# Explicit places for recurrence steps, evacuations and side work, and the x sums of the first half on GpSimd, in a retention and HGRN2 inference step

## The chip, the cores and the metric

The kernel runs on one core of a Trainium2 chip. The metric is the device time of one execution in microseconds (us), median over several; the profile comes from one execution. TensorE (PE; PEld is its weight load) multiplies matrices, VectorE (DVE), ScalarE (ACT) and GpSimd (POOL) work element by element, SyncE (SP) only issues DMAs. Each engine runs its own instructions in one fixed order and waits on semaphores for the others.

## The reference

One layer on 2048 prompt tokens (and 8 single-token samples with stored states): normalise, project to eight groups of 512 columns, run four retention heads and four HGRN2 heads of 128 x 128 state, gate, project back, add the input, normalise.

```python
h = rmsnorm(x, norm_g)
p = (h @ w_in).astype(jnp.float32)
rq, rk, rv, rg, hq, hf, hi, hgate = jnp.split(p, 8, axis=-1)
rq, rk = rotary(rq, pos), rotary(rk, pos) * RET_DK ** -0.5
o_ret, s_ret_new = chunked_decay_recurrence(rq, rk, rv, log_gamma, s_ret)    # S = g S + k v, o = S q
o_ret = head_rmsnorm(o_ret, ret_g) * silu(rg)
logf = logaddexp(log(lb), log1p(-lb) + log_sigmoid(hf));  kin = (1 - lb) * sigmoid(-hf)
o_hg, s_hg_new = chunked_decay_recurrence(silu(hq), kin, hi, logf, s_hg)     # one decay per key row
o_hg = head_rmsnorm(o_hg, hg_g) * silu(hgate)
y = rmsnorm(x + concatenate([o_ret, o_hg], -1) @ w_out, final_norm_g)
```

All matrix products with weights are in float32 by two parts each: a high part that TensorE takes exactly and the low rest; high x high, high x low and low x high are added.

## The kernel before, in words

**Products.** Big matrix products are done in 2 x 2 blocks by a scheme of Strassen's kind with seven products per unit (`SLOTS`: A11, S1, S2, S4, A12, S3, A22 against B11, T1, T2, B22, B21, T3, T4). One product is 4 x 3 = 12 matmuls of 128x128 by 512 columns. S are sums of blocks of the one operand, T sums of blocks of the other.

**Units and positions.** Time is counted in positions; unit `u` begins at position 7u, and each whole position holds one product in two halves (the last product of a unit stands at 9, in the next unit). After a start in plain form, units -6 to -1 make V (values, stored to `v_dram`). Units 0 to 23 are the scan: H, G, R in turn (HGRN forget gate and query; both gates; retention key and query) for heads 0 to 3, first for tokens 0 to 1023 (units 0 to 11), then for 1024 to 2047. Units 24 to 31 are the output projection O, 256 tokens each. So three scan units, 21 positions, belong to one head of each kind. Units 0 to 11 write their split weights for H and R to `w_dram`; units 12 to 23 read them back (`w_reload`).

**x.** In V the normalised tokens are one operand in blocks (`tok_ops`: normalise, split in high and low, sums S1 to S4). For the scan they are the other operand: 1024 tokens as B11, B21, B12, B22 and T1 to T4. B11 and B21 stay from the last V units; `x12_load`, `x_norm`, `x_t1` to `x_t4` load and normalise the other 512 tokens once more and make T1 to T4 and B22 on VectorE with ScalarE's high parts. For the second half (`x1_*`) this is done in small steps during the first half and kept in `x_dram`, from which `swap_load` and `x_split` fetch it; the output weights' sums (`wo_*`, `t_dram`) likewise.

**Recurrences.** An H or R unit is followed by its recurrence over 8 chunks of 128 tokens. HGRN (`hgrn_rec`): `scores0`, `scores(1)`, `scores(3)`, `scores3` build the score matrix A level by level (TensorE's small matmuls, then `update` on VectorE, `keep`'s copies on ScalarE, the next `update`). Both kinds then share `tail_steps`, with g = 0, 1 for four chunks each: `kt` transposes keys, `uu` makes the state updates, `oo` the outputs (then four squares on ScalarE with accumulated sums, `rsqrt_mean` on GpSimd, four scalings on ScalarE into `ob`), `tr` transposes `ob`, multiplies by the gate on VectorE and stores to `o_dram`. Tiles `A`, `st`, `ks` and `ob` have one buffer each, `ps_lv` and `ps_o` two banks.

**Order.** `at(pos, f)` collects all steps, which are sorted by position and emitted. This order is binding for TensorE alone (`manual_schedule` with TensorE); for the other engines and the DMA queues a planner chooses at build time, by its own estimates, which instruction goes next. Recurrence steps are spread over a stretch by weights:

```python
for n, w in enumerate(ws):
    s += w
    at(7 * u + lo + (hi - lo) * s / total + 0.25, lambda n=n: get(n))
```

with 11.5 to 20.0 for HGRN (weights total 13.9) and 11.3 to 17.8 for retention (5.6). Work tiles of 128x512 come from a list of 12 (`t_get`, `t_done`), split weights from a ring of 6 (`r_get`, `r_done`); both lists hand out what was freed longest ago.

Of the kernel before, what the change touches and what calls it, by code (L numbers as in the profile page):

```python
# [18 lines left out]
P = 128  # L19
# [20 lines left out]
N_OB = 1  # L40
# [6 lines left out]
def step_kernel(ctx, tc, a, out):  # L47
# [27 lines left out]

    ident = const.tile([P, P], F32, name="ident")
# [4 lines left out]
    pool.memset(mhalf, -0.5)  # L81

# [6 lines left out]
    warm = const.tile([P, 1], F32, name="warm")  # L89
    act.activation(warm, zero[:, 0:1], AF.Sigmoid)  # L90
# [13 lines left out]
    lbd = const.tile([P, NH], F32, name="lbd")  # L104
    lb = const.tile([P, NH], F32, name="lb")
    lb1 = const.tile([P, NH], F32, name="lb1")
    lmask = const.tile([P, len(SMALL) * 16], U8, name="lmask")
    rs_all = const.tile([P, T // P], F32, name="rs_all")
    rsd = const.tile([NB, 2], F32, name="rsd")
# [26 lines left out]
    t_tag = {}  # L136

    def t_get(shape, name, dtype=F32):
        if not t_free:
            raise RuntimeError(f"{name}: " + " ".join(str(t[1].tensor.name) for t in t_tag.values()))  # L140
        tag = t_free.pop(0)
        t = tp.tile(shape, dtype, tag=tag, name=name)
        t_tag[id(t)] = (tag, t)
        return t
# [14 lines left out]
    V_ORDER = [4, 5, 6, 7, 2, 3, 0, 1]  # L159
# [36 lines left out]
    def stats(i):  # L196
        p = V_ORDER[i]
        ms = sm.tile([P, 4], F32, tag="ms", name=f"ms{p}")
        for j in range(2):
            c = 2 * p + j  # L200
            for h in range(2):
                r = t_get([P, GW], f"xn{c}{h}")
                sp.dma_start(r, a["x_prompt"][0, c * P : (c + 1) * P, h * GW : (h + 1) * GW])
                act.activation(r, r, AF.Square, accum_out=ms[:, 2 * h + j : 2 * h + j + 1])  # L204
                t_done(r)
        pool.tensor_tensor(ms[:, 0:2], ms[:, 0:2], ms[:, 2:4], op=ALU.add)  # L206
        rsqrt_mean(rs_all[:, 2 * p : 2 * p + 2], ms[:, 0:2], D, EPS)
# [20 lines left out]

    def tok_ops(i):
        r0, r1 = xr[i]  # L230
        rb = spread_to[i]
        for j, r in enumerate((r0, r1)):
            for k in range(4):
                kk = 4 * j + k
                dve.scalar_tensor_tensor(  # L235
                    r[:, k], r[:, k], g_in[:, kk : kk + 1], rb, op0=ALU.mult, op1=ALU.mult
                )
            n = P if i < 6 and j == 0 else 2 * P
            at = slice((i % 2) * 256, (i % 2) * 256 + n)
            hi_lo(x0[j][0][:, :, at], x0[j][1][:, :, at], r[:, :, :n])  # L240
        a11, a21, a12, a22 = r0[:, :, :P], r0[:, :, P:], r1[:, :, :P], r1[:, :, P:]
        s1, s2, s3, s4 = (t_get([P, 4, P], f"{n}_{i}") for n in ("S1", "S2", "S3", "S4"))
        dve.tensor_tensor(s1, a21, a22, op=ALU.add)
        dve.tensor_tensor(s2, s1, a11, op=ALU.subtract)
        dve.tensor_tensor(s3, a11, a21, op=ALU.subtract)
        dve.tensor_tensor(s4, a12, s2, op=ALU.subtract)
        sraw[i] = dict(S1=s1, S2=s2, S3=s3, S4=s4)

    sraw = {}

    def s_split(i, n):
        t, src = r_get(f"s{i}{n}"), sraw[i][n]
        split_raw(t, src.rearrange("p k t -> p (k t)"))
        t_done(src)
# [201 lines left out]
    r4 = {}  # L456

    def x12_load(kp):
        r4[kp] = rawp.tile([P, 2, 512], F32, tag="raw", name=f"xr1{kp}")
        for j in range(2):  # L460
            sp.dma_start(r4[kp][:, :, j * 256 : j * 256 + 256], a["x_t"][2 + j, :, 2 * kp : 2 * kp + 2])

    def blk_dg(blk, dg):
        dve.tensor_tensor(
            dg, ident.unsqueeze(1).to_broadcast([P, 4, P]),
            rs_all[:, 4 * blk : 4 * blk + 4].unsqueeze(2).to_broadcast([P, 4, P]), op=ALU.mult,
        )

# [5 lines left out]

    xs_box = {}

    def x_dg():
        xs_box["dg"] = t_get([P, 4, P], "dgb1")
        blk_dg(1, xs_box["dg"])

    def x_spread():
        xs_box["rb"] = t_get([P, GW], "rbb1")
        blk_spread(1, xs_box["dg"], xs_box["rb"])
        t_done(xs_box["dg"])

    def x_norm(kp):
        for j in range(2):
            k = 2 * kp + j
            dve.scalar_tensor_tensor(
                r4[kp][:, j], r4[kp][:, j], g_in[:, k : k + 1], xs_box["rb"], op0=ALU.mult, op1=ALU.mult  # L490
            )
# [21 lines left out]

    def x_block(b, src):
        h, l = x_tile(b, "x")
        halves(lambda kk, n: hi_lo(h[:, kk], l[:, kk], src[n]))

    def x_t1():
        b11 = [t.bitcast(F32) for t in X["B11"]]
        halves(lambda kk, n: sub(r4[n], r4[n], b11[1][:, kk]))  # L520
        halves(lambda kk, n: sub(r4[n], r4[n], b11[0][:, kk]))
        x_block("T1", r4)

    def x_t2():
        for n in range(2):
            sub(r4[2 + n], r4[2 + n], r4[n])
        x_block("T2", [r4[2], r4[3]])

    def x_t3():
        b11 = [t.bitcast(F32) for t in X["B11"]]  # L530
        halves(lambda kk, n: sub(r4[n], r4[2 + n], b11[0][:, kk]))
        halves(lambda kk, n: sub(r4[n], r4[n], b11[1][:, kk]))
        x_block("T3", r4)

    def x_t4():
        b21 = [t.bitcast(F32) for t in X["B21"]]
        halves(lambda kk, n: sub(r4[2 + n], b21[1][:, kk], r4[2 + n]))
# [1034 lines left out]
```

## Time and profile before

| what | value |
| --- | --- |
| median of 3 runs | 1182.38 us (1181.15 to 1185.52) |
| the profiled execution's own time | 1185.04 us |
| its span, first to last instruction | 1183.3 us |
| mean granted TensorE clock | 0.951 |
| DMA | 226.71 MB, mean 192 GB/s |

In the profile a group's line gives the source line, the engine, the operation, the tile written and the tiles read, shapes, count, then busy time and the mean duration, then the idle time of the engine just before these instructions and what ended it. "PE poth L884 <- ACT obh L876: 22.4, 8, 6.4" says that TensorE waited 22.4 us in 8 times, at most 6.4, before it wrote `poth` in line 884, until ScalarE's `obh` of line 876 was there. Names ending in h belong to HGRN, in r to retention.

### The profile page before, as it was taken

How to read it: one execution, taken by the hardware profiler on the slowest of the kernel's cores; microseconds unless marked ns; L12 is line 12 of the kernel's file. 1: busy time of each engine (PE TensorE's matmuls, PEld its weight loads, DVE VectorE, ACT ScalarE, POOL GpSimd, SP SyncE). 2: the span in 40 equal slices, each digit the busy share in tenths (PEclk: the TensorE clock that was granted, in tenths of full speed). 3: DMA queues.
4: the chain of work that ended last, by engine and by line, in shares of the span. 5: the costliest groups of instructions: out<-in, count | busy, mean ns of one | idle time of the engine just before them, and what ended most of it. 6: DMA issues, size and time to landing. Idle time of an engine off the chain costs nothing.

```text
span 1183.3 us, 22553 instructions
## 1 busy us (share of the span) xinstructions
PE 1070.9 (91%) x8696; PEld 867.4 (73%) x8696; DVE 786.1 (66%) x1366; ACT 579.8 (49%) x1316; POOL 233.6 (20%) x379
## 2 busy tenths in 40 slices
PE   9999996998898899889799979879998799999997
PEld 7777884777766777677677758657786677778886
DVE  7767598676666666677676446635655468977774
ACT  7745353555445455455574435425444448543342
POOL 2401000023122222312102112111211411031111
PEclk9999997998999999999989989979998899999999
DMA  8554445277456736755786654765564179544431
GB/s 308 198 170 146 140 160 186 105 263 266 153 198 237 255 140 236 254 184 179 284 277 193 209 195 154 221 200 191 170 225 146 30 233 322 193 131 166 152 125 71
DMA packets 126555, 226.71 MB, mean 192 GB/s; under 512 B 11200, under 2 KB 67648, under 8 KB 124656
## 3 DMA queue, kind: packets, MB, share of 16 engines
q1 hardware_dynamic: 104496, 150.52, 39.8%
q0 software_dynamic: 21808, 74.50, 16.5%
q8 instruction: 68, 1.11, 0.4%
q14 instruction: 39, 0.32, 0.1%
q10 hardware_dynamic: 144, 0.26, 0.1%
HBM read 141.81 MB, written 83.43 MB: 190 GB/s over the span
## 4 chain that ended last, share of the span: by engine, by line
PE 45%; DMA 16%; DVE 13%; issue 12%; POOL 6%; ACT 5%; SPq 1%; DVEq 0%; POOLq 0%; ACTq 0%
PE aO L689 6%; PE aH L689 5%; PE aV L689 4%; DMA g_dram<-g 3%; PE aG L689 3%; PE eO L689 3%; PE aR L689 3%; DMA dv<-vd_dram 2%; DMA wo<-in_w_out 2%; PE eG L689 2%; PE eH L689 2%; PE eV L689 2%; PE bO L689 2%; PE bR L689 1%; DMA xn<-in_x_prompt 1%
## 5 line engine op out<-in xcount | busy, mean ns | idle before, releaser
L973 ACT ACTIVATE qh<-kh 128x1024 f32<-128x1024 f32 x24 | 25.5, 1061 | 45.6 <-DVE kh L961 45.6
L961 DVE TENSOR_TENSOR kh<-kh,fph 128x512 f32<-128x512 f32 x48 | 33.0, 687 | 6.0 <-PE plh L1038 2.8
L868 PE MATMUL poh<-sth,qt 128*128 128x128 f32 x112 | 24.0, 297 | 14.1 <-DVE sth L859 14.0
L1226 DVE TENSOR_TENSOR dv<-dv,dk 128x512 f32<-128x512 f32 x16 | 11.0, 690 | 38.2 <-DMA dv<-vd_dram 38.1
L1342 DVE SCALAR_TENSOR_TENSOR xro<-xro,yms,fg 128x1024 f32<-128x1024 f32 (+1 forms) x17 | 20.7, 1222 | 22.9 <-POOL yms L117 21.5
L884 PE MATMUL poth<-ident,obh 128*128 128x128 f32 x64 | 15.4, 349 | 22.4 <-ACT obh L876 22.4
L876 ACT ACTIVATE obr<-por,orsr 128x128 f32<-128x128 f32 x64 | 18.2, 368 | 35.5 <-POOL orsr L117 35.5
L204 ACT ACTIVATE xn<-xn 128x512 f32<-128x512 f32 x32 | 20.0, 625 | 30.4 <-DMA xn<-in_x_prompt 27.4
L763 POOL DMA_DIRECT2D g_dram<-g x32 | 17.4, 542 | 86.5 <-DVE g L762 84.8
L1333 ACT ACTIVATE yj<-xro 128x512 f32<-128x512 f32 x32 | 20.3, 633 | 28.8 <-DVE xro L509 28.0
L872 ACT ACTIVATE obh<-poh 128x128 f32<-128x128 f32 x64 | 16.7, 275 | 34.9 <-PE poh L868 19.2
L964 DVE TENSOR_TENSOR qt<-qt,fph 128x512 f32<-128x512 f32 x48 | 33.1, 689 | 0.0
L235 DVE SCALAR_TENSOR_TENSOR xr<-xr,g_in,prs 128x256 f32<-128x256 f32 x48 | 19.8, 476 | 19.2 <-PE prs L224 19.2
L761 ACT ACTIVATE sg<-g 128x512 f32<-128x512 f32 x32 | 20.1, 628 | 25.2 <-DVE g L509 24.8
L884 PEld LDWEIGHTS poth<-ident,obh 128*128 128x128 f32 x64 | 9.9, 162 | 30.1 <-ACT obh L876 25.9
L206 POOL TENSOR_TENSOR ms<-ms 128x2 f32<-128x2 f32 x8 | 10.5, 1314 | 100.3 <-ACT xn L204 100.3
L868 PEld LDWEIGHTS poh<-sth,qt 128*128 128x128 f32 x112 | 18.0, 202 | 15.8 <-DVE sth L859 15.8
L762 DVE SCALAR_TENSOR_TENSOR g<-g,pk,sg 128x512 f32<-128x512 f32 x32 | 23.9, 748 | 6.3 <-ACT sg L761 5.8
L876 ACT ACTIVATE obh<-poh,orsh 128x128 f32<-128x128 f32 x64 | 18.2, 368 | 17.6 <-POOL orsh L117 17.6
L916 PE MATMUL par<-qr,kr 128*128 128x128 f32 x128 | 18.0, 285 | 9.6 <-DVE qr L509 9.6
L916 PEld LDWEIGHTS par<-qr,kr 128*128 128x128 f32 x128 | 17.1, 198 | 12.4 <-DVE qr L509 10.9
L866 PE MATMUL poh<-vh,A 128*128 128x128 f32 x128 | 25.5, 287 | 0.4
(1607 smaller groups left out, 3818.7 us busy)
## 6 DMA issues: line engine op xcount, KB each, us to landing
xn<-in_x_prompt SPq DMA_DIRECT2D x32, 256.0 KB, 4.0
v_dram<-vo SPq DMA_DIRECT2D x32, 256.0 KB, 4.1
g_dram<-g POOLq DMA_DIRECT2D x32, 256.0 KB, 4.5
xro<-in_x_prompt SPq DMA_DIRECT2D x16, 512.0 KB, 3.3
out_y_prompt<-xro POOLq DMA_DIRECT2D x15, 512.0 KB, 3.0
xr<-in_x_t SPq DMA_DIRECT2D x12, 512.0 KB, 4.7
t_dram<-wo POOLq DMA_DIRECT2D x20, 256.0 KB, 3.2
vh<-v_dram SPq DMA_DIRECT2D x16, 256.0 KB, 3.4
```

What stands on the lines that cost most here:

```text
L689: pe.matmul(ps, w[i], x[j], start=(first and k == 0 and m == 0), stop=(k == 3 and m == 2), skip_group_check=True,)
L762: dve.scalar_tensor_tensor(y, y, ng[:, hd : hd + 1], sg, op0=ALU.mult, op1=ALU.mult)
L866: pe.matmul(po[:, j], s_ctx["A"][:, c], box["v"][g][:, j], start=True, stop=src is None)
L868: pe.matmul(po[:, j], qcol(c), src, start=False, stop=True)
L876: act.activation(ob[:, j], po[:, j], AF.Copy, scale=rs[:, j : j + 1])
L884: pe.transpose(pt[:, j], box["ob", g][:, j], ident)
L916: pe.matmul(pa[:, j], k[:, cc], q[:, cc], start=True, stop=True)
L961: dve.tensor_tensor(kv[:, :, 0, :], kv[:, :, 0, :], two[:, :, 1:2].to_broadcast([P, nb, b]), op=ALU.mult)
L964: dve.tensor_tensor(qv[:, :, 1, :], qv[:, :, 1, :], two[:, :, 0:1].to_broadcast([P, nb, b]), op=ALU.mult)
L973: act.activation(kept_k, k, AF.Copy)
L1333: act.activation(jk, xro[c][:, (LO, HI)[n]], AF.Square, accum_out=yms[c][:, n : n + 1])
L1342: dve.scalar_tensor_tensor(xro[c][:, cc], xro[c][:, cc], ms[:, 0:1], fgb["t"][:, cc], op0=ALU.mult, op1=ALU.mult)
```

## The change

1. All events go to a heap, and `after(d, f)` puts a later part of a step `d` positions behind it. The whole loop is emitted under `manual_schedule` for VectorE, ScalarE, GpSimd and SyncE as well: their instructions and DMAs go in the order of the source, that is, of the positions. (What stands ahead of the loop stays with the planner, except on TensorE.)
2. Recurrence steps get positions of their own (`REC`), HGRN over 12.0 to 28.6 and retention over 11.9 to 20.1; retention's scores come ahead of its key transposes. `kt` takes its bank from `ps_lv`. Roots, scalings, stores, gates, rotations and copies follow by `after`. `ob` has two buffers.
3. The blocks B12 and B22 of the first half's x are stored while V normalises them (`tok_spool`); `V_ORDER` ends with 0, 1, 2, 3 where it ended with 2, 3, 0, 1, so the first half's kept blocks are tokens 512 to 1023, and `TB = (1, 0)` swaps the token halves everywhere in the scan. GpSimd makes T1 to T4 in pieces of 128x512 in the last two V units (`blocks_sums`) and stores them to `x_dram`; `swap_load` fetches them from position -6.4 on, with splits from -3.6 to 7.3. `x12_load`, `x_dg`, `x_spread`, `x_norm`, `x_block`, `x_t1` to `x_t4` go.
4. One of the ring's six buffers becomes two more work tiles when the scan opens; loads and side work (decode, x of the second half, output weights) get other positions; copies of unsummed output weights go from DRAM to DRAM (`wo_copy`, on SyncE's queue) and no longer from the work tile on GpSimd's queue.

```diff
-N_OB = 1
+N_OB = 2
+TB = (1, 0)
-    V_ORDER = [4, 5, 6, 7, 2, 3, 0, 1]
+    V_ORDER = [4, 5, 6, 7, 0, 1, 2, 3]
...
+    def at(pos, f):
+        count[0] += 1
+        heapq.heappush(ev, (pos, count[0], f))
+    def after(d, f):
+        at(now[0] + d, f)
...
+    def blocks_sums(i, n):
+        b11, b21 = (r[:, 2 * n : 2 * n + 2] for r in xr[i])
+        b12, b22 = (bs.pop((i, n, b)) for b in ("B12", "B22"))
+        t1, t2 = (t_get([P, 2, 256], f"b{t}{i}{n}") for t in ("T1", "T2"))
+        def put(b, t):
+            after(0.4, lambda: pool.dma_start(x_dram[X_NAMES.index(b), :, 2 * n : 2 * n + 2, slot(i)], t))
+            after(0.41, lambda: t_done(t))
+        def less(o, x, y):
+            pool.tensor_tensor(o, x, y, op=ALU.subtract)
+        less(t1, b12, b11)
+        put("T1", t1)
+        less(t2, b22, t1)
+        put("T2", t2)
+        less(b12, b22, b12)
+        put("T3", b12)
+        less(b22, b21, t2)
+        put("T4", b22)
...
     def scan_open():
+        big = wp.tile([P, 2, GW], F32, tag=free.pop(), name="big")
...
-            rsqrt_mean(rs, ms, P, eps)
-            for j in range(4):
-                act.activation(ob[:, j], po[:, j], AF.Copy, scale=rs[:, j : j + 1])
+            def root():
+                rsqrt_mean(rs, ms, P, eps)
+            def scale():
+                for j in range(4):
+                    act.activation(ob[:, j], po[:, j], AF.Copy, scale=rs[:, j : j + 1])
+            after(0.5, root)
+            after(1.0, scale)
...
-            update(li)
+            after(0.35, copies)
+            after(1.1, lambda: update(li))
...
-            for n, name in zip((-3.4, -2.4, -0.4, 0.6, 1.6, 2.6, 3.6), W_NAMES):
+            for n, name in zip((-3.4, -2.4, -1.4, -0.4, 0.6, 1.6, 2.6), W_NAMES):
                 at(U + n, lambda name=name: w_reload(u, name))
...
+    REC = {
+        0: (("s0", 12.0), ("s1", 14.8), ("s2", 17.6), ("load", 18.0), ("s3", 20.2), ("k0", 21.7), ("u0", 23.0),
+            ("k1", 23.2), ("o0", 23.9), ("u1", 24.3), ("o1", 25.1), ("last", 25.5), ("t0", 27.2), ("t1", 28.6)),
+        2: (("s0", 11.9), ("load", 12.0), ("s1", 12.7), ("k0", 13.3), ("u0", 14.3), ("k1", 14.5), ("o0", 15.5),
+            ("u1", 15.9), ("o1", 17.2), ("last", 17.6), ("t0", 18.8), ("t1", 20.1)),
+    }
-    REC_W = {
-        0: (0, 0.3, 2.3, 2.3, 2.3, 1.9, 0.9, 0.2, 0.5, 0.7, 0.9, 0.9, 0.7, 0),
-        2: (0, 0.3, 0.3, 0.6, 0.3, 0.3, 0.8, 0.6, 0.8, 0.8, 0.8, 0),
-    }
...
+    swap_events(0, "x0", dict(T1=-6.4, T2=-4.8, B22=-3.4, T3=-2.0, T4=-0.4),
+                dict(T1=-3.6, T2=-1.4, B22=0.8, T3=2.8, T4=6.8))
...
-        p0 = 84 + 7.2 + (0, 7.5, 14.2, 21.0, 28.5, 35.2, 42.0, 49.5)[hd]
-        at(p0, lambda hd=hd: d_load(hd))
+        p0 = 84 + 7.2 + (3.0, 10.2, 16.5, 21.9, 29.0, 35.5, 42.6, 49.5)[hd]
+        at(p0 - 2.5, lambda hd=hd: d_load(hd))
-    at(151.1, d_ms)
-    at(153.1, d_od)
+    at(158.0, d_ms)
+    at(163.1, d_od)
...
-    ev.sort(key=lambda e: e[:2])
-    for _, _, f in ev:
-        f()
+    with tc.manual_schedule(engines=ORDERED):
+        while ev:
+            now[0], _, f = heapq.heappop(ev)
+            f()
```

More of the change, by code (lines that the diff above doesn't have):

```diff
@@ L1 @@
+import heapq
 from contextlib import ExitStack
@@ L1142, in step_kernel, with wo_copy @@
     wd = {}
+    def wo_copy(k):
+        for b in ("B11", "B21", "B22"):
+            kh, n = int(b[1]) - 1, int(b[2]) - 1
+            sp.dma_start(
+                t_dram[X_NAMES.index(b), :, k], a["w_out"][(4 * kh + k) * P : (4 * kh + k + 1) * P, n * GW : (n + 1) * GW]
+            )
     def wo_load(k):
@@ L1150, in wo_sums, with put, store @@
     def wo_sums(k):
-        def put(b, t, keep=False):
-            pool.dma_start(t_dram[X_NAMES.index(b), :, k], t)
-            if not keep:
+        def put(b, t):
+            def store():
+                pool.dma_start(t_dram[X_NAMES.index(b), :, k], t)
                 t_done(t)
+            after(0.4, store)
         t1, t2 = t_get([P, GW], f"woT1{k}"), t_get([P, GW], f"woT2{k}")
-        put("B11", wd[0, 0], True)
-        put("B21", wd[1, 0], True)
-        put("B22", wd[1, 1], True)
         sub(t1, wd[0, 1], wd[0, 0])
         t_done(wd[0, 0])
-        put("T1", t1, True)
         sub(wd[0, 1], wd[1, 1], wd[0, 1])
@@ L1174, in swap_load @@
         x_tile(b, kind)
[L1175 removed]
+        sp.dma_start(raw(b), (t_dram if kind == "wo" else x_dram)[X_NAMES.index(b)])
     def flat(t):
```

452 lines of the change are left out of this document (236 added, 216 removed).

## The prediction

> **What bounds the kernel now.** I read the page first, then busy times by stage, then who waits for whom on TensorE, then the granted clock around one wait.
>
> ```profile
> span 1183.3 us, 22553 instructions
> PE 1070.9 (91%) x8696; PEld 867.4 (73%) x8696; DVE 786.1 (66%) x1366; ACT 579.8 (49%) x1316; POOL 233.6 (20%) x379
> PEclk9999997998999999999989989979998899999999
> ...
> ```
>
> TensorE is busy for 91% and no other engine for more than 66%: the time is TensorE's work, plus its idle time, plus whatever the low clock adds. By stage (V products and start; first and second half of the scan; output stage):
>
> ```profile
> 0.00:195.00 195.00, 181.69 (x826) 145.46 (x826) 148.13 (x252) 105.24 (x211) 27.93 (x38) 0.98 0.52 177
> 195.00:600.00 405.00, 359.12 (x3625) 289.63 (x3626) 272.75 (x493) 211.42 (x488) 96.91 (x163) 0.94 0.62 216
> 600.00:1030.00 430.00, 385.60 (x3590) 314.01 (x3589) 261.33 (x474) 207.34 (x486) 77.52 (x108) 0.94 0.61 196
> 1030.00:1184.00 154.00, 144.49 (x658) 118.36 (x656) 103.88 (x150) 55.81 (x132) 31.20 (x70) 0.98 0.39 131
> ...
> ```
>
> Columns: stretch, length, busy PE, PEld, DVE, ACT, POOL, clock, DMA. Idle TensorE time is 13.3, 45.9, 44.4 and 9.5 us (the last mostly the final output leaving). The clock is 0.94 in the scan.
>
> ```profile
> PE poth L884 <- ACT obh L876: 22.4, 8, 6.4
> PE poh L868 <- DVE sth L859: 14.0, 7, 4.9
> PE potr L884 <- ACT obr L876: 10.7, 6, 2.8
> PE aV L689 <- DVE vo L509: 9.7, 3, 7.3
> PE par L916 <- DVE qr L509: 9.6, 3, 3.6
> PE pkh L838 <- DVE kh L961: 9.5, 3, 4.3
> PE pur L848 <- ACT ksr L840: 8.0, 1, 8.0
> PE plh L1033 <- ACT fh L974: 4.9, 3, 2.3
> PE aH L689 <- DVE vo L509: 4.1, 1, 4.1
> ...
> ```
>
> Nearly all of the scan's idle time is TensorE standing in its own fixed order before a step of a recurrence whose operand is still in a chain over VectorE, ScalarE and GpSimd. No wait here is for a weight load or for a block evacuation of the scan's products. The two `vo` rows are the seam between V products and scan.
>
> ```profile
> 331.51 1.10 PE L884 MATMUL potr<-ident,obr 128*128 128x128 f32 x4 [1.85 <-ACT obr L876]
> ...
> 332.90:336.30 3.40, 3.40 (x30) 2.00 (x24) 1.86 (x4) 0.04 (x1) 0.54 (x1) 0.50 0.58 193
> ...
> ```
>
> After a wait of 1.85 us the clock is 0.50 for the next 3.4 us, with TensorE busy throughout: a short wait costs itself and about 1.7 us more. The Trainium skill, "TensorE: Matmul & The Clock Gate", section "Why this matters for your kernels", advises to avoid idle gaps of more than about 3 us; here a shorter one was enough. By that rule the leftover waits below would cost no clock and the sum would be some 7 us lower; the row decides.
>
> **The change, term by term.**
>
> *Floor.* Scan idle: 45.9 + 44.4 = 90.3 us. Scan low clock: 835 us x 0.06 = 50 us; I take 43, since the clock also falls while the longest waits still last. Seam: the two waits 7.3 and 4.1 with about 5 us of half clock behind them, 16 us. If all this goes, the span is 1183.3 - 90 - 43 - 16 = 1034 us. TensorE's instructions hardly change (`x_spread`, 4 small matmuls, goes; bank tags differ).
>
> *Seam: the x sums.* Before, VectorE makes T1, T2, T3, T4 in one piece in the last V unit:
>
> ```profile
> 158.00:200.00 42.00, 30.56 (x146) 23.77 (x146) 41.33 (x48) 16.41 (x22) 2.10 (x4) 0.88 0.41 147
> ...
> L489 DVE SCALAR_TENSOR_TENSOR xr<-xr,g_in,rbb 128x512 f32<-128x512 f32 x8 | 5.6, 747 | 0.5 <-DMA xr<-in_x_t 0.3 <-ACT rbb L473 0.2
> L512 DVE TENSOR_TENSOR xr<-xr,x0B11l 128x1024 f32<-128x1024 f32 x4 | 4.7, 1220 | 0.0
> L512 DVE TENSOR_TENSOR xr<-xr,x0B11h 128x1024 f32<-128x1024 f32 x4 | 4.7, 1219 | 0.0
> ...
> ```
>
> VectorE is busy 41.3 of 42 us there. The 8 norms (5.6 us) go, as the V loop's normalised rows are kept in DRAM; 14 subtractions or additions of 1.22 us (the 8 shown and 6 of the same form), 17 us, leave VectorE. GpSimd does 16 subtractions of 128x512 instead, 8 in each of the last two V units. No row has such an instruction. Low end: VectorE's rate, 1.22 / 2 = 0.6 us. High end: GpSimd's widest row,
>
> ```profile
> L1269 POOL TENSOR_TENSOR dsq<-dsq,mhalf 128x64 f32<-128x64 f32 x1 | 10.6, 10550 | 0.1
> L206 POOL TENSOR_TENSOR ms<-ms 128x2 f32<-128x2 f32 x8 | 10.5, 1314 | 100.3 <-ACT xn L204 100.3
> ...
> ```
>
> scaled to 512 columns, 84 us each; that row is a power, and a subtraction is nearer to the addition of L206, so I take its 1.3 us plus 0.6 for streaming, 2 us: 16 us of GpSimd per V unit. The `blocks_sums` of block 7 stand at -9.0 and -8.2, the first product that needs T1 at 1.0. A product is
>
> ```profile
> 102.69 2.72 PE eV L689 x12
> ...
> 993.16 7.38 DMA woB21l<-t_dram
> ...
> x_dram<-x1B POOLq DMA_DIRECT2D x16, 256.0 KB, 4.3
> ...
> ```
>
> so 10 positions are 27 us. Out of these go a store to `x_dram` (4.3 us), a 1 MB load like the one shown (7.4 us) and two splits of 1.22 us, which leaves 13 us for the five sums up to T1, 2.6 us each. At 2 us it is hidden. T2, B22, T3, T4 have 2 to 8 positions more. The splits now stand at -3.6, -1.4, 0.8, 2.8, 6.8 rather than together. The new traffic (4 stores of 0.5 MB, 8 loads and 16 stores of 0.25, 5 loads of 1: 13 MB, against 2 MB of `x12_load`) meets DMA at 0.41; it can make one load late: 0 to 10 us, I take 2.
>
> *Recurrences.* A position holds one product, 2.72 us, plus what recurrence steps fall into it.
>
> ```profile
> L973 ACT ACTIVATE qh<-kh 128x1024 f32<-128x1024 f32 x24 | 25.5, 1061 | 45.6 <-DVE kh L961 45.6
> L961 DVE TENSOR_TENSOR kh<-kh,fph 128x512 f32<-128x512 f32 x48 | 33.0, 687 | 6.0 <-PE plh L1038 2.8
> L872 ACT ACTIVATE obh<-poh 128x128 f32<-128x128 f32 x64 | 16.7, 275 | 34.9 <-PE poh L868 19.2
> L872 ACT ACTIVATION_READ_ACCUMULATOR obh<-poh 128x1 f32 x8 | 1.6, 206 | 0.0
> L876 ACT ACTIVATE obh<-poh,orsh 128x128 f32<-128x128 f32 x64 | 18.2, 368 | 17.6 <-POOL orsh L117 17.6
> L974 ACT ACTIVATE fh<-qt 128x512 f32<-128x512 f32 x3 | 1.9, 630 | 0.0
> L117 POOL TENSOR_TENSOR orsh<-orsh,mhalf 128x4 f32<-128x4 f32 x16 | 17.4, 1088 | 1.2
> ...
> ```
>
> Output chain: four squares with reads 4 x 0.48 = 1.9, roots 1.1 + 0.3 to 0.5, four scalings 1.5: some 5 us, more with hand-overs and behind one `ob` buffer. From `o1` to `t1` of HGRN TensorE had 1.6 weights of 13.9 over 8.5 positions, 0.98 position (2.7 us of products): hence `poth`. Now it has 3.5 (9.5 us), and `N_OB` is 2; retention goes from 1.9 to 2.9. Covered.
> Score steps: update 2 x 0.69, copies 1.06 + 0.63, update 1.4, after 1.2 us of matmuls: 5.7 us. Spacing was 1.41 positions, is 2.8 and 2.6 (7 us of products, 8 to 9 with the rest). Covered while VectorE is on time.
> State and output (`poh`, `pkh`): 1.5 positions from `s3` to `k0` for 1.16, 0.8 from `u1` to `o1` for 0.55. Covered by less.
> `par`: with `TB` swapped, the token half that comes last (position 9.5, rotation at 10.3) is first read by `s1` at 12.7. Covered.
> `pur`, once: behind the 10.55 us power between `d_ms` and `d_od`, 2.0 positions apart before, 5.1 now (13.9 us). Covered.
>
> *VectorE as the cover.* In source order each engine executes what position says, so a burst delays all behind it. I added VectorE's instructions by position over a cycle of 21 in the first half: 70 us (75 with an x1 and an output-weight step) against TensorE's 88. The worst burst is position 12 to 14 (`s0`, its updates and products, two gates, two evacuations, six weight steps, a transposed output):
>
> ```profile
> L954 DVE TENSOR_TENSOR fph<-fph 128x256 f32<-128x256 f32 (+5 forms) x6 | 1.5, 244 | 0.1
> L762 DVE SCALAR_TENSOR_TENSOR g<-g,pk,sg 128x512 f32<-128x512 f32 x32 | 23.9, 748 | 6.3 <-ACT sg L761 5.8
> ...
> ```
>
> 14 instructions of 0.69 (updates, first product, weights, evacuations, output), 2 gates of 0.75, six products of 1.5 in all, two short ones of about 0.4: 13.5 us on VectorE, against 8.2 on TensorE (four half products 5.4, `s0` 1.2, the rest 1.6). The backlog is 5.3 us, still 4 us at `s1` (14.8), gone at 18. So `s1` to `s2` is 1 us short: in each of four first-half groups 1 us of wait and 1.7 of half clock, 11 us in all. In the second half, with two of three units reloading their weights, I find at most 2.4 us of backlog: 1 us a group, 4 us. The ring loses a buffer (5 left): by the positions of splits and of products ending, at most 5 are alive, hence 0.
>
> *GpSimd and SP queues.* Stores and roots stand 0.4 to 1.2 positions behind their producers, so their queue rarely stands; the wider leads of `d_load` and of the output-weight loads are hidden. `wo_copy` reads DRAM twice: hidden at 0.61 DMA.
>
> *Output stage.* `y_out` is unchanged, but VectorE can no longer put another instruction ahead of it.
>
> ```profile
> L1342 DVE SCALAR_TENSOR_TENSOR xro<-xro,yms,fg 128x1024 f32<-128x1024 f32 (+1 forms) x17 | 20.7, 1222 | 22.9 <-POOL yms L117 21.5
> ...
> ```
>
> It waits 1.3 us each time; if that doubled, a unit would hold 103.9 / 154 x 19 = 12.8 us of work and 5.4 of wait in 19 us. 0 to 8 us; I take 3.
>
> *Sum.* 1034 + 2 + 11 + 4 + 3 = 1054 us of span; the profiled execution took 1185.0 us with its 1183.3 us of span, 2.7 us above the median of 1182.4, so about 1053 us as a median.
>
> **The rivals.**
> 1. *Half of the scan's waits stay* (VectorE's backlog is longer than the added positions cover: hand-overs between engines are not in my sums, and VectorE stands in order before every evacuation and split). For it: 85% load in the first half, 0.8 position between `u1` and `o1`. 1053 + 133 / 2 - 15 = 1105 us.
> 2. *GpSimd's sums hold VectorE off* in the last two V units: 16 us each on top of VectorE's (148 - 23) / 195 x 20 = 13 us, in 20: 9 us over, twice, with 1.7 of clock each: 1053 + 21 = 1074. The traces have no wide GpSimd instruction to show it. The Trainium skill, "SBUF — State Buffer", section "Who interferes with whom", says that a VectorE instruction with two SBUF inputs and a GpSimd one that reads SBUF exclude each other for a whole instruction; no run so far shows it.
> 3. *Slower: roots come late on GpSimd.* Its queue is now in order too; a `w_dram` store ahead of a root waits for VectorE's low part of a split, ScalarE then stands at the scalings, and evacuations behind it. There are 32 roots. With VectorE's 5.3 us backlog at each, 170 us: 1223 us. It decides from 130 / 32 = 4 us of TensorE wait a root. Against it: ahead of a retention root no weight store stands within five positions; ahead of the first HGRN root one does, by 0.2.
> 4. *It doesn't do what it says*: the waits move to the next step of the same chain, and only the seam is won: 1166 us.
>
> **How the numbers follow.** Forecast 0.54 (1035 to 1070), rival 1 0.22, rival 2 0.07, rival 4 0.06, within 0.5% of before 0.03, slower 0.08 (rival 3, or sums on GpSimd near the far end). 0.5% is about what a measurement of this kernel can tell from no change. Range 1035 to 1125 us: from the floor to the far side of rival 1, with rival 2 inside and rivals 3 and 4 left out. Faster 0.89, same 0.03, slower 0.08.
>
> **What would show it.** Right: PEclk 9 or more in all slices, idle TensorE below 30 us, no `poth`, `par` or `pur` row of more than 5 us; no wait for `vo` at the seam; TensorE busy about the same in the output stage. Rival 1: `plh`, `poh` or `pkh` rows as now. Rival 2: VectorE's subtractions longer or late around the last V units. Rival 3: ScalarE's rows `obh`, `obr` waiting on GpSimd longer than now, and TensorE on evacuations. Wrong at the root: TensorE busy time that doesn't fall although its idle time does.

## The result, and the profile after

The changed kernel takes 1064.92 us (median of 4, 1060.14 to 1067.49), 0.900 of the time before (95% interval 0.895 to 0.904). The forecast was 1053 us, the range 1035 to 1125. The profiled execution took 1067.5 us with a span of 1065.7. One of four executions of the kernel before, of 5714.76 us, is not counted.

First the page of the changed kernel (span, engines, granted clock in 40 slices):

```profile
span 1065.7 us, 22525 instructions
PE 1023.8 (96%) x8688; PEld 842.2 (79%) x8688; DVE 776.7 (73%) x1343; ACT 567.5 (53%) x1315; POOL 262.9 (25%) x403
PEclk9999999999999999999999999999999998999999
```

Then its busy times by stage, in the columns used before (stretch, length, busy PE, PEld, DVE, ACT, POOL, clock, DMA share, GB/s); the third stretch ends 154 us ahead of the end, so that the output stage is as long as before:

```profile
0.00:195.00 195.00, 189.23 (x862) 152.23 (x863) 138.60 (x232) 101.50 (x212) 70.04 (x76) 0.99 0.68 238
195.00:600.00 405.00, 390.48 (x4144) 322.05 (x4142) 311.78 (x557) 242.46 (x558) 99.67 (x168) 0.98 0.71 245
600.00:912.00 312.00, 298.83 (x3017) 248.58 (x3017) 219.03 (x397) 169.00 (x411) 63.86 (x89) 0.98 0.68 228
912.00:1066.00 154.00, 145.22 (x670) 119.32 (x667) 107.25 (x159) 54.55 (x137) 29.35 (x71) 0.99 0.41 139
```

TensorE's idle time (length less busy) is 5.8, 14.5, 13.2 and 8.8 us, 42 in all, where it was 13.3, 45.9, 44.4 and 9.5, 113 in all: 71 us saved. Its busy time fell from 1070.9 to 1023.8 us, by 47 us, with the same matrix products. Most of that is half clock: by the mean granted clock (0.951 and 0.986) the two kernels lose 1183.3 x 0.049 = 58 us and 1065.7 x 0.014 = 15 us to it, 43 us apart. 71 + 47 = 118 us is the difference of the spans. The clock is 0.98 in the scan, where it was 0.94.

Who TensorE waits for (us in total, times, longest):

```profile
PE pdp L632 <- ACT obh L933: 5.8, 3, 1.9
PE prs L263 <- DVE dg L256: 3.6, 2, 2.9
PE plh L1055 <- issue: 3.1, 2, 2.3
PE plh L1110 <- DVE qth L1023: 3.0, 1, 3.0
PE poh L921 <- DVE sth L912: 3.0, 1, 3.0
PE pd L1330 <- ACT obh L933: 2.1, 1, 2.1
...
```

`poth`, `potr` and `par` are gone, `vo` is down to 0.2 us, `poh` fell from 14.0 in 7 times to 3.0 in one. The longest row, `pdp`, was not among the waits of before: it is the decode of the single-token samples, whose matmuls take a bank that ScalarE must first have emptied (line 933, the scalings of the outputs `poh`).

**Where that wait comes from.** The trace of the changed kernel, one of the three times, instructions in order of time (start, duration, engine, line, operation, then in brackets the idle time ahead of it and what ended it):

```profile
366.03 0.55 POOL L1177 DMA_DIRECT2D x_dram<-big  x1 [4.12 <-DVE big L1172]
...
366.65 0.19 POOL L128 TENSOR_SCALAR orsh<-omsh 128x4 f32<-128x4 f32 x1
366.93 1.03 POOL L129 TENSOR_TENSOR orsh<-orsh,mhalf 128x4 f32<-128x4 f32 x1
...
368.00 1.14 ACT L933 ACTIVATE obh<-poh,orsh 128x128 f32<-128x128 f32 x4 [5.52 <-POOL orsh L129]
```

```profile
369.19 0.43 PE L632 MATMUL pdp<-big,xz 128*32 128x128 f32 x8 [1.94 <-ACT obh L933]
```

A store of the second half's x (`x1_two`, block B22) stands in GpSimd's order right ahead of HGRN's root. It waits 4.1 us for VectorE to normalise the block; the root behind it, ScalarE's scalings behind the root (5.5 us) and TensorE's decode behind the scalings wait in turn. The clock behind this wait and behind another (same columns as the stages):

```profile
369.90:373.30 3.40, 3.40 (x9) 2.62 (x10) 1.74 (x3) 3.33 (x9) 2.95 (x5) 0.50 0.80 290
719.60:723.00 3.40, 3.40 (x32) 2.87 (x33) 1.35 (x2) 3.33 (x13) 1.22 (x2) 1.00 0.92 278
```

The wait of 1.94 us at 367 us is followed by 3.4 us at half clock; the one of 2.12 us at 717 us (`pd`) is not. The third row of the waits stands for one wait above all, in the middle of a group of small matmuls:

```profile
515.17 0.24 PE L1055 MATMUL plh<-qth,kh 128*32 128x16 f32 x5 [2.28 <-issue]
```

VectorE had made the group's operands `kh` and `qth` by 510.98 us, so this is not a wait for VectorE; the profile names no releaser. It is followed by 3.4 us at half clock as well (0.51 from 516.6 to 520.0 us).

**The seam.** GpSimd's sums (line 334) take 1.26 to 2.30 us each, 25.8 us for the 16. While they run, some of VectorE's instructions are long. VectorE from 120 to 165 us (groups by line and form: busy us, mean ns of one, idle us before them):

```profile
L272 DVE SCALAR_TENSOR_TENSOR xr<-xr,g_in,prs 128x256 f32<-128x256 f32 x16 | 6.6, 470 | 0.0
L172 DVE TENSOR_TENSOR s6S<-S,s6S 128x512 fp32r<-128x512 f32 x4 | 5.9, 1467 | 2.6 <-ACT s6S L171 2.6
L133 DVE TENSOR_TENSOR x0B11l<-xr,x0B11h 128x1024 fp32r<-128x1024 f32 x2 | 3.8, 1899 | 0.0
L256 DVE TENSOR_SCALAR dg<-ident,rs_all 128x128 f32<-128x128 f32 x2 | 2.5, 1290 | 0.0
```

The experiment `e3_dve_sums` below has the rows to compare them with: 687 ns for `s6S` and 1214 for `x0B11l`. `dg` (267 to 483 ns there, up to 1298 here) is what the row `prs <- dg` waits for.

**End of the scan.** VectorE stands before a sum of the output weights (`r24S`) whose rows come late:

```profile
861.77 0.69 DVE L585 TENSOR_TENSOR r24S<-big,r24A 128x512 f32<-128x512 f32 x1 [4.31 <-DMA r24A<-o_dram]
```

Behind it in VectorE's order are the updates `kh` and `qth` of the last HGRN group; TensorE waits 2.98 us for `qth`, 16 us later 2.97 us for `sth`, and runs 3.4 and 6.8 us at half clock behind the two. From 861.8 us until `sth`, at 882.3, VectorE has no idle time. Experiments 5 and 7 show that the first wait hangs on the load and the second doesn't.

### The profile page after: what moved, and what is told of

Read it like the earlier page. It is cut to its first block, busy times and chain, and to the rows that moved or that the text cites. A ratio compares the mean times of both kernels' runs of the same rounds, so it can differ in the third digit from the quotient of the medians.

```text
span 1065.7 us, 22525 instructions
## 1 busy us (share of the span) xinstructions
PE 1023.8 (96%) x8688; PEld 842.2 (79%) x8688; DVE 776.7 (73%) x1343; ACT 567.5 (53%) x1315; POOL 262.9 (25%) x403
## 4 chain that ended last, share of the span: by engine, by line
PE 69%; DVE 9%; DMA 7%; issue 6%; POOL 4%; ACT 3%; SPq 0%; POOLq 0%; DVEq 0%; ACTq 0%
PE aO L724 7%; PE aG L724 6%; PE aR L724 6%; PE aH L724 6%; PE pv L365 4%; PE eG L724 4%; PE eR L724 4%; PE aV L724 3%; PE eO L724 3%; PE eH L724 2%; PE bH L724 2%; PE eV L724 2%; PE bO L724 2%; PE plh L1055 1%; PE bG L724 1%
## 5 line engine op out<-in xcount | busy, mean ns | idle before, releaser
L1422 ACT ACTIVATE yj<-xro 128x512 f32<-128x512 f32 x27 | 17.1, 633 | 74.6 <-DVE xro L573 38.4
L1431 DVE SCALAR_TENSOR_TENSOR xro<-xro,yms,fg 128x1024 f32<-128x1024 f32 (+1 forms) x17 | 20.7, 1222 | 31.8 <-POOL yms L129 29.8
L933 ACT ACTIVATE obr<-por,orsr 128x128 f32<-128x128 f32 x64 | 18.3, 369 | 27.8 <-POOL orsr L129 27.8
L1023 DVE TENSOR_TENSOR qth<-qth,fph 128x512 f32<-128x512 f32 x48 | 32.8, 684 | 0.0
L948 POOL DMA_DIRECT2D o_dram<-gth x16 | 8.9, 558 | 93.3 <-DVE gth L946 93.3
L128 POOL TENSOR_SCALAR orsh<-omsh 128x4 f32<-128x4 f32 x16 | 3.8, 236 | 107.4 <-ACT obh L925 107.1
L925 ACT ACTIVATE obr<-por 128x128 f32<-128x128 f32 x64 | 16.7, 275 | 24.7 <-PE por L921 24.7
L933 ACT ACTIVATE obh<-poh,orsh 128x128 f32<-128x128 f32 x64 | 18.0, 364 | 21.7 <-POOL orsh L129 21.7
L754 ACT ACTIVATE vo<-aV 128x512 f32<-128x512 f32 x12 | 7.1, 591 | 39.5 <-PE aV L724 30.9
L808 POOL DMA_DIRECT2D g_dram<-g x29 | 15.8, 544 | 44.1 <-DVE g L804 42.6
L921 PE MATMUL poh<-sth,qth 128*128 128x128 f32 x112 | 22.6, 284 | 3.0 <-DVE sth L912 3.0
L912 DVE SCALAR_TENSOR_TENSOR sth<-sth,fph,puh 128x128 f32<-128x128 f32 x48 | 16.6, 345 | 12.1 <-PE puh L901 10.7
L919 PE MATMUL por<-vr,A 128*128 128x128 f32 x128 | 24.0, 274 | 0.0
L573 DVE TENSOR_TENSOR xro<-aO,xro 128x512 f32<-128x512 f32 x33 | 22.5, 684 | 1.4 <-PE aO L724 1.2
```

The costliest lines, as they stand in the source:

```text
L573: dve.tensor_tensor(o, x, y, op=ALU.add)
L919: pe.matmul(po[:, j], s_ctx["A"][:, c], box["v"][g][:, j], start=True, stop=src is None)
L921: pe.matmul(po[:, j], qcol(c), src, start=False, stop=True)
L925: act.activation(ob[:, j], po[:, j], AF.Square, accum_out=ms[:, j : j + 1])
L933: act.activation(ob[:, j], po[:, j], AF.Copy, scale=rs[:, j : j + 1])
L1023: dve.tensor_tensor(qv[:, :, 1, :], qv[:, :, 1, :], two[:, :, 0:1].to_broadcast([P, nb, b]), op=ALU.mult)
```

## The experiments

Ratios are to the kernel before, run on the same chip in the same series (changed kernel: 0.8997). A kernel that is ordered by the planner keeps TensorE's fixed order.

**1. The places without the order.** All parts of the change, but VectorE, ScalarE, GpSimd and SyncE go back to the planner.

```diff
-    with tc.manual_schedule(engines=ORDERED):
-        while ev:
-            ...
+    while ev:
+        ...
```

> The changed kernel with all its places, but VectorE, ScalarE, GpSimd and SyncE are ordered by the planner again, as before the change; TensorE's order stays. Theory A (TensorE's wider places do it: a chain has 2 to 3.5 positions where it had 1 to 1.5, whoever orders the other engines): 1060 to 1090 us, low clock below 50 us in all. Theory B (the explicit order of the other engines does it): 1120 us or more, with poth, poh, par back among TensorE's waits.

Measured: 1113.15 us, 0.9405 [0.938, 0.943], between the numbers of the two theories: both have a part. Everything but the order brings 0.06, about 70 us, and the order adds 0.04, about 48 us. Of the rows that theory B names `poh` is back (15.8 us in two rows), `poth` and `par` are not. The waits of this run:

```profile
PE aV L724 <- DVE vo L573: 10.7, 2, 6.1
PE poh L921 <- DVE sth L912: 8.3, 6, 2.3
...
PE aH L724 <- DVE kr L573: 6.2, 1, 6.2
PE pds L1341 <- ACT do L1337: 4.7, 1, 4.7
...
```

The seam's wait for `vo` is here as before the change, with the sums on GpSimd and the splits at their new positions: neither took it away by itself; with the order it went.

**2. The order without the places.** The recurrence steps at the places of before (HGRN `s0` 11.93, `s1` 13.34, `s2` 14.75, `s3` 16.15, `k0` 17.31 to `t1` 20.25, retention 11.55 to 18.05 with `k0` ahead of `s0`), roots, scalings and gate loads 0.3, 0.6 and 0.7 behind where they stood 0.5, 1.0 and 1.2.

```diff
-    REC = {0: (("s0", 12.0), ("s1", 14.8), ("s2", 17.6), ..., ("t1", 28.6)), 2: (..., ("t1", 20.1))}
+    REC = {0: (("load", 11.75), ("s0", 11.93), ("s1", 13.34), ("s2", 14.75), ..., ("t1", 20.25)), 2: (..., ("t1", 18.05))}
-            after(0.5, root)
-            after(1.0, scale)
+            after(0.3, root)
+            after(0.6, scale)
```

> The changed kernel with the recurrence steps at the places they had before (HGRN over 11.75 to 20.25, retention over 11.55 to 18.05, in the old sequence) and roots, scalings and gate loads at 0.3, 0.6 and 0.7 positions instead of 0.5, 1.0 and 1.2; explicit order of all engines, two ob buffers and the sums on GpSimd stay. Theory A: most of the scan's waits come back, 5 to 9 us of wait and as much half clock a group of three units, 8 groups: 1120 to 1180 us. Theory B: below 1095 us.

Measured: 1158.27 us, 0.978 [0.974, 0.982], in theory A's range; it is faster than the kernel before, but whether by 2% its interval leaves open.

```profile
PE plh L1055 <- DVE qth L1023: 28.8, 8, 5.3
PE poth L944 <- DVE gth L946: 19.9, 7, 5.7
PE pur L901 <- DMA vr<-v_dram: 14.5, 6, 3.8
...
```

The order with the old spacing brings 0.022, the spacing without the order 0.06, both 0.10, each time with the rest of the change (sums, loads, side work, two `ob` buffers). What that rest brings by itself was not run, so how far the two help each other can't be read from these numbers. Each adds to the other: the spacing 0.078 on top of the order, the order 0.041 on top of the spacing. A reading that fits, but is not shown, is that TensorE's fixed order leaves the chains room only where the steps are apart, and that the room is used only where the other engines come to the chain in time. The rows above are what the new places removed: 28.8 us before the score steps and 19.9 before the transposed outputs.

Only the offsets of that edit, with the new places:

> The changed kernel with roots, scalings and gate loads at 0.3, 0.6 and 0.7 positions behind the outputs (the offsets of e2), all else as changed: what e2 owes to these offsets alone. Theory A (the spacing of the recurrence steps made e2 slow): 1060 to 1072 us. Rival (ScalarE stands at scalings whose roots are not ready, and that made e2 slow): 1090 or more.

Measured: 1064.84 us, 0.8964 [0.893, 0.900]. That can't be told from the changed kernel: the offsets are worth nothing here, and the run before this one speaks for the places. But the trace is another one. The roots 0.3 behind the outputs come ahead of the store of x (at 360.03 us, the store at 366.25), and all three `pdp` waits are gone; `pur` waits 3.4 us in their place (1.2 in the changed kernel), `plh <- issue` 4.5 (3.1), `plh <- qth` 3.9 (3.0).

**3. Which recurrence pays.** The tight places for one kind at a time, with the offsets of experiment 2 for both.

> Only HGRN's recurrence steps at their old, tight places; retention's at the new ones; explicit order on all engines. In the run with both tight, rows that belong to HGRN (plh, poth, with qth and gth) held about 56 us of TensorE's waits, rows of retention (pur, potr, pkr) about 27, and that run was 93 us slower than the changed kernel. Theory 'each kind pays for its own spacing': the 93 us split 2 to 1, so about 1065 + 63 = 1128 us here. Rival 'one late step delays the other kind through the shared in-order engines': either kind alone brings most of the loss, here 1140 us or more, with waits in retention's rows too.

> Only retention's recurrence steps at their old places and in their old sequence (key transposes ahead of the scores); HGRN's at the new ones; explicit order on all engines. Theory 'each kind pays for its own spacing': about 1065 + 30 = 1095 us, waits in pur, potr and pkr alone. Rival 'shared in-order engines': 1120 us or more, with plh and poth waits.

Measured: HGRN tight 1134.09 us, 0.9563 [0.952, 0.960]; retention tight 1085.23 us, 0.915 [0.911, 0.919]. Against the changed kernel 0.057 and 0.015, together 0.072 of the 0.078 that both cost. The first time lies between the theory's 1128 us and the rival's 1140, the second below the theory's 1095. The waits with HGRN tight, then with retention tight:

```profile
PE plh L1055 <- DVE qth L1023: 23.3, 8, 4.0
PE poth L944 <- DVE gth L946: 22.1, 8, 5.7
PE pur L901 <- ACT ksr L893: 7.9, 6, 1.9
...
```

```profile
PE par L976 <- DVE A L977: 6.7, 3, 3.1
PE pkr L891 <- DVE str L912: 5.3, 5, 3.7
...
```

Each kind mostly pays for itself; `pur`, a row of retention, waits 7.9 us in the first run although its own places are untouched. The split is 4 to 1, not the 2 to 1 expected: `pur <- vr` (14.5 us in experiment 2) was counted as retention's own; it is 0.9 us with retention tight and absent with HGRN tight, so it takes both.

**4. The sums on VectorE.**

```diff
-            pool.tensor_tensor(o, x, y, op=ALU.subtract)
+            dve.tensor_tensor(o, x, y, op=ALU.subtract)
```

> The 16 subtractions of blocks_sums on VectorE instead of GpSimd, nothing else moved. If taking them off VectorE is what opens the seam: 16 x 0.69 = 11 us more on VectorE in the last two V units, the waits for vo come back and it is 8 to 16 us slower than the changed kernel, 1073 to 1081. If doing them early and in pieces is what opens it: VectorE then holds 13 + 5.5 us in a V unit of 20, all hidden, and its subtractions no longer stretch to 1.2 to 1.8 us: 1058 to 1066 us, the prs wait of 2.9 us gone.

Measured: 1060.43 us, 0.8955 [0.893, 0.898], not to be told from the changed kernel by time alone. VectorE from 120 to 165 us in this run:

```profile
L272 DVE SCALAR_TENSOR_TENSOR xr<-xr,g_in,prs 128x256 f32<-128x256 f32 x16 | 6.6, 474 | 0.0
...
L172 DVE TENSOR_TENSOR s6S<-S,s6S 128x512 fp32r<-128x512 f32 x4 | 2.7, 687 | 1.4 <-ACT s6S L171 1.4
L133 DVE TENSOR_TENSOR x0B11l<-xr,x0B11h 128x1024 fp32r<-128x1024 f32 x2 | 2.4, 1214 | 0.0
...
```

Two numbers beside each other: subtractions with both inputs in SBUF go from 1467 to 687 and from 1899 to 1214 ns, while the one that reads a PSUM input (`prs`) stays at 470 and 474. The waits for `dg` are gone, and TensorE's idle time in the first 195 us falls from 5.8 to 1.9 us with no half clock left. This is rival 2's mechanism. Of the two theories the second holds, in the time and in the waits: moving the sums to GpSimd isn't what opens the seam. Doing them early and in pieces was not run apart from the order. The Trainium skill, "SBUF — State Buffer", section "Who interferes with whom", names a VectorE instruction with two SBUF inputs and a GpSimd one that reads SBUF as a pair that excludes each other; the trace agrees, with 1467 against 687 ns. A sum is 0.69 us on VectorE.

**5. The store out of the root's way**, on top of 4; then also the rows of unit 24 two positions earlier.

```diff
-        x1_put("B22", k, True)
+        t = xd["B22"]
+        after(1.0, lambda: pool.dma_start(x_dram[X_NAMES.index("B22"), :, k], t))
```
```diff
-            at(U + {0: -7.6, 1: -8.6}.get(u, -5.2) + 0.5 * n, lambda name=name: w_load(u, name))
+            at(U + {0: -7.6, 1: -8.6, 24: -7.2}.get(u, -5.2) + 0.5 * n, lambda name=name: w_load(u, name))
```

> The changed kernel with the sums on VectorE (as e3) and with the store of the normalised B22 in x1_two put one position later, so that it no longer stands in GpSimd's queue ahead of the roots of HGRN's first output. If the store ahead of the root is what makes ScalarE late at the scalings and TensorE at pdp: the three pdp waits of 1.94 us and their half clock of 1.7 us each go, 1060 - 11 = 1049 us (1046 to 1054). If the bank is late for another reason (VectorE's norm itself): 1058 to 1062.

> e4 and the four loads of the first output unit's o_dram blocks two positions earlier (-7.2 instead of -5.2 before unit 24). If VectorE standing 4.3 us in order for that load is what delays the last HGRN recurrence's update and state: the waits plh 2.8 and poh 2.7 and about 5 us of half clock there go, 10 us less than e4 (1036 to 1043). If the load is late by its queue (SyncE stands at reloads ahead of it), it comes no earlier: same as e4 within 3 us.

Measured: 1052.93 us, 0.8873 [0.884, 0.890], and 1048.44 us, 0.8839 [0.881, 0.887]. With the store moved the same place of the trace reads (GpSimd, then TensorE):

```profile
354.68 1.03 POOL L129 TENSOR_TENSOR orsh<-orsh,mhalf 128x4 f32<-128x4 f32 x1
358.49 0.62 POOL L1201 DMA_DIRECT2D x_dram<-big  x1 [2.77 <-DVE big L1172]
```

```profile
359.60 0.43 PE L632 MATMUL pdp<-big,xz 128*32 128x128 f32 x8
```

The store still waits, but behind the root, and TensorE doesn't: all three `pdp` waits and the half clock behind them are gone, 3 x (1.94 + 1.7) = 11 us by the trace and 0.8955 - 0.8873 = 0.008, 9.7 us, by the times. The earlier rows of unit 24 take VectorE's wait for them away, and `plh <- qth` at the end of the scan falls to 0.6 us; `poh <- sth` stays, with 2.5 us. At the same place a wait of 2.96 us before `aO` on VectorE's `kr` came up with 6.8 us of half clock (in the profiled execution, the longest of the six with 1055.19 us); the two intervals overlap, so no gain is shown.

**6. Which engines' order matters.** `ORDERED` with VectorE and ScalarE alone; with GpSimd and SyncE alone.

> The changed kernel with only VectorE and ScalarE in the order of the source; GpSimd's and SyncE's queues are the planner's. If VectorE's and ScalarE's order is what the explicit order brings: 1060 to 1075. If the queues of stores, roots and loads matter as much: 1085 to 1115.

> The changed kernel with explicit order on GpSimd and SyncE alone (beside TensorE); VectorE and ScalarE ordered by the planner. With the planner on all four the time was 1113 us, with the order on VectorE and ScalarE alone 1050, on all four 1065. Theory 'the two orders act apart: VectorE and ScalarE gain 63, the queues of GpSimd and SyncE lose 14': 1113 + 14 = 1127 us. Rival 'the order of the queues costs only because ordered producers come late': no more than 1113 us. Rival 'GpSimd's order is part of the gain': below 1105 us.

| order of VectorE, ScalarE | order of GpSimd, SyncE | us | ratio |
| --- | --- | --- | --- |
| planner | planner | 1113.15 | 0.9405 [0.938, 0.943] |
| planner | source | 1093.56 | 0.9206 [0.916, 0.925] |
| source | planner | 1050.42 | 0.8837 [0.880, 0.887] |
| source | source | 1064.92 | 0.8997 [0.895, 0.904] |

In the last run the two theories by which the queues' order is never a gain fell, and the third, that it is part of the gain, was right: the two orders don't add up. The order of GpSimd and SyncE gains 0.020 where the planner orders VectorE and ScalarE, and loses 0.016 where these are ordered. Of the loss, 19 us by the ratios, experiment 5 puts 10 to 11 us down to a store ahead of roots, and experiment 7 finds more stores of that kind. For the gain of 0.020 I only have that `aH <- kr` falls from 6.2 us in experiment 1 to 0.8 and that `pds <- do` (4.7) is absent; what removed them wasn't sought.

**7. The best pair, and which queue costs.** The order on VectorE and ScalarE alone with the sums on VectorE:

```diff
-    mybir.EngineType.DVE, mybir.EngineType.Activation, mybir.EngineType.Pool, mybir.EngineType.SP,
+    mybir.EngineType.DVE, mybir.EngineType.Activation,
```

> Explicit order on VectorE and ScalarE only, and the x sums of the first half on VectorE instead of GpSimd. The run with that order alone kept two seam waits, prs<-dg 4.6 and aV<-vo 4.0 us, with 6.8 us of half clock behind them: 12 us. Theory 'GpSimd's sums stretch VectorE's instructions and these waits go with them': 1050 - 12 = 1038 us. Rival 'only prs<-dg goes, the vo wait is VectorE's own load': 1044 us. Rival 'at the planner's order of GpSimd and SyncE the sums cost nothing, and VectorE gets 11 us more work in the seam': 1050 us or more.

Measured: 1041.12 us, 0.8773 [0.874, 0.880], the fastest kernel here, halfway between the first theory's 1038 us and the first rival's 1044; the waits decide. In the run with that order alone the longest waits were

```profile
PE prs L263 <- DVE dg L256: 4.6, 1, 4.6
PE aV L724 <- DVE vo L573: 4.0, 1, 4.0
```

The first is gone and the second down to 0.5 us, so that wait for `vo` too hung on the sums. The engines and the longest waits of the best kernel (VectorE doesn't stand for the load of `r24A` in it):

```profile
PE 1013.0 (97%) x8688; PEld 835.0 (80%) x8688; DVE 776.5 (75%) x1359; ACT 567.4 (55%) x1315; POOL 237.4 (23%) x387
```

```profile
PE poh L921 <- DVE sth L912: 3.7, 1, 3.7
PE aH L724 <- DMA w12A<-w_dram: 2.3, 1, 2.3
...
```

Then GpSimd in order as well, with the store moved as in 5, and SyncE alone left to the planner:

> Explicit order on VectorE, ScalarE and GpSimd, SyncE ordered by the planner, the first half's x sums on VectorE, and x1_two's store of B22 one position later. Two runs stand beside it: all four ordered with the same two edits took 1053 us, and neither GpSimd nor SyncE ordered (sums on VectorE) took 1041. Theory 'with the store moved, GpSimd's order costs nothing, the rest is SyncE's: loads behind others in its queue, o_dram's above all': 1041 to 1044 us, no wait plh<-qth at the end of the scan. Rival 'GpSimd's order still costs it': 1050 to 1053 us, with the wait.

Measured: 1050.66 us, 0.886 [0.883, 0.889]. The time is the rival's, but not by the wait that the rival named: the loads for `r24S` were issued from 806.5 to 819.9 us, in the changed kernel from 846.9 to 850.9, and `plh <- qth` at the end of the scan is gone. The loss is at other places. First GpSimd in this run, then in the one before (the best):

```profile
699.06 0.76 POOL L1319 DMA_DIRECT2D out_new_hgrn_sample<-dS  x1 [10.67 <-DVE dS L573]
706.46 0.77 POOL L1319 DMA_DIRECT2D out_new_hgrn_sample<-dS  x1 [6.63 <-issue]
707.30 0.19 POOL L128 TENSOR_SCALAR orsh<-omsh 128x4 f32<-128x4 f32 x1
```

```profile
692.43 0.76 POOL L1318 DMA_DIRECT2D out_new_hgrn_sample<-dS  x1 [10.65 <-DVE dS L573]
693.52 0.49 POOL L128 TENSOR_SCALAR orsh<-omsh 128x4 f32<-128x4 f32 x1 [0.33 <-ACT obh L925]
694.09 1.03 POOL L129 TENSOR_TENSOR orsh<-orsh,mhalf 128x4 f32<-128x4 f32 x1
700.78 0.84 POOL L1318 DMA_DIRECT2D out_new_hgrn_sample<-dS  x1 [5.65 <-issue]
```

Two stores of new sample states, 7 to 8 us apart, stand ahead of a root in source order; the planner put the root between them. TensorE then waits 3.5 us for the scalings (`pd`; 2.1 us in the changed kernel, where the same two stores stand ahead of the root). A second place is VectorE:

```profile
684.53 0.69 DVE L576 TENSOR_TENSOR woT<-wo,big 128x512 f32<-128x512 f32 x1 [4.00 <-DMA g_dram<-g]
```

The store of `g` that it waits for was issued at 675.91 us, right behind a store of a new sample state for which GpSimd stood 6.8 us; in the best kernel the planner put it ahead of that store, at 667.59, and VectorE doesn't wait. TensorE waits 2.6 us for the `kh` that follows. The third place, 2.8 us before `plh` at 500 us with 6.8 us of half clock behind it, again has no releaser. By the trace the first two places cost 3.5 + 1.7 and 2.6 + 1.7 us with their half clock. So GpSimd's order costs 9 to 10 us even with the x store moved, and SyncE's nothing that can be seen beside it (0.886 against 0.8873).

## Why the prediction was right or wrong, point by point

- **The bound** was as read: idle time before recurrence steps and the half clock behind it. Both parts shrank (taken: 90 and 43 us in the scan and 16 at the seam, with 20 given back; measured: 71 and 47 us), and no other engine or transfer became the bound.
- **The floor, 1034 us.** It kept 11 us of idle time outside the scan; the changed kernel has 14.6 there, 3.6 of it at the seam. As a bound it holds: the best kernel's span is 1040.8.
- **The step that was mis-sized is the idle time left in the scan.** The sum had 15 us for it with its clock, from VectorE's backlog at `s1` and in the second half. The stages show 14.5 + 13.2 = 27.7 us of idle time alone, and behind six of the waits some 12 us of half clock. Part of the idle time are waits of 1.3 us and less (`pds`, `pur`, `pkh`), each of which the sum took at nothing.
- **The reason given for those 15 us fell in the first half.** There `plh` waits for `qth` only twice, for 0.3 us each, so the backlog of 5.3 us at positions 12 to 14 was covered; the step from `s1` to `s2` was not short. With the tight places the same wait came to 28.8 us. What filled the term instead is 3 x (1.94 + 1.7) = 11 us from a store ahead of a root, 2.3 + 1.7 = 4 us before `plh` at 515 us without a releaser, and 3.0 + 1.7 us at the end of the scan with a late load ahead of updates on VectorE.
- **For the second half the backlog was too small.** The sum found at most 2.4 us on VectorE and took 4 us. The wait for `sth` at the end of the scan cost 3.0 + 3.4 us by itself. It isn't the load's: it stays, with 2.5, 3.7 and 3.4 us, in the runs of experiments 5 and 7 in which VectorE doesn't stand for that load. In the best kernel VectorE is idle for less than 1 us of the 22 us ahead of `sth`, with sums of the output weights and rotations, which reads as its own backlog; no run moved that work.
- **"Stores and roots stand 0.4 to 1.2 positions behind their producers, so their queue rarely stands"** was wrong in this sense: rival 3's mechanism is there, in four places of 32 (three `pdp`, one `pd`), with 2 us each. ScalarE's wait for HGRN's roots rose from 17.6 to 21.7 us, the one for retention's fell from 35.5 to 27.8. The text on rival 3 counts the weights' stores to `w_dram` alone; the stores that mattered were those of the side work, `x_dram` and the new sample states. The price of 4 us a root from which that rival decides was far off.
- **Rival 2** (sums hold VectorE off) was treated as another way to go, with 21 us. It was true along with the forecast, and cost 3.6 + 1.7 = 5 us; the seam's 2 us had been put down to a late load, and TensorE waits for none there. A sum was taken at 2 us and is 1.6 in the mean (25.8 / 16).
- **Rivals 1 and 4** are excluded: of 90 us of idle time in the scan 28 stay, and more than the seam is won. Of rival 1's rows `poh` and `pkh` fell to 3.0 and 1.8 us, `plh` only from 8.8 to 6.7 over all its rows. Something of rival 4 is there: `pdp` and `pd` wait 7.9 us for the scalings that `poth` waited for before. Experiment 2 is close to what rival 4 describes: there the waits stay in the chain.
- **The output stage** was given 3 us. VectorE's wait for GpSimd's root grew from 21.5 to 29.8 us, but TensorE is busy 145.2 of 154 us (144.5 before): 0.
- **What would show it.** Right: no `poth`, `par`, `pur` row of over 5 us, no `vo` of more than 0.2 us at the seam, the output stage unchanged, TensorE's busy time falling with its idle time. Not right: one slice of the clock is 8, and idle time is 42, not below 30.
- **A wait costs itself and 1.7 us.** Right for the waits of 1.94, 2.28, 2.94 and 2.98 us; the 2.97 us before `sth` cost 3.4, and the 2.12 us of `pd` cost no clock.
- **Part of the change worked against it.** The order of GpSimd and the sums on GpSimd were both losses here: without them the kernel takes 1041 us. What gained is the order of VectorE and ScalarE (0.057 on top of the planner's 0.9405) together with the places, HGRN's above all (0.057, retention's 0.015). Part 4 of the change, the kept blocks of part 3 and the second `ob` buffer have no run of their own.

Open: TensorE's waits of 2 to 3 us before `plh` (line 1055) near 500 us, for which the profile names no releaser; the wait for `sth` at the end of the scan; what the rest of the change brings without order and places; and the gain of the queues' order with a planner on VectorE and ScalarE.

## What to carry to other kernels

Where one engine's order is fixed and others feed it, spread the steps of a dependent chain and let the feeding engines keep the same order; here, each with the rest of the change, the order brought 0.022, the places 0.06 and both 0.10. Before an in-order queue is trusted, list every store on it that stands right ahead of a small instruction of the critical chain, those of the side work first: its producer's delay passes to that chain. Read the trace even where the time is unchanged: in `e6_offsets` the longest wait was gone and others had taken its place. An idle engine is no free place for work if its instructions lengthen those of the loaded one; look at the mean duration of the same line with and without it.

## What the runs showed of the hardware that was not expected

- A GpSimd subtraction of 128x512 took 1.26 to 2.30 us (0.69 on VectorE), and lengthened VectorE's two-input subtractions by up to 2.1 times in the mean of a group (687 to 1467 ns). `dg`, which scales one matrix by a column, was held as well: up to 1298 ns, where it took at most 483 with the sums on VectorE.
- Half clock after a wait came in stretches of 3.4 or 6.8 us; 1.94 us sufficed for it three times and 2.28 us once, 2.12 us once didn't, nor did 2.3 us in the best kernel (the stretch behind its `aH` wait):

```profile
512.60:516.00 3.40, 3.40 (x18) 2.79 (x18) 0.57 (x1) 2.63 (x4) 0.00 (x0) 1.00 1.01 419
```

The Trainium skill, "TensorE: Matmul & The Clock Gate", section "Why this matters for your kernels", advises to keep gaps below about 3 us; these rows have shorter ones that did cost clock and some that didn't.
